# Queue orders in a two-layer RWKV-7 and gated-MLP trunk: w_o splits, LoRA weights, block weights

## The chip, the cores and the metric

The kernel runs on one core of a Trainium2 chip. The metric is the device time of one execution, in microseconds (us). A core has five engines with a queue each, worked off in order: PE (TensorE: matmuls and transposes), DVE (VectorE), ACT (ScalarE), POOL (GpSimd) and SP (SyncE, which here issues nearly all DMAs). Engines wait for one another by semaphores only, so an instruction that waits holds up everything behind it in its own queue.

## The reference

Input x is (1, 512, 1024) in float32. Two layers, each a token mixer and a dense feed-forward part, each with an RMS norm in front and another behind it:

```python
for i in range(DEPTH):                       # 2
    h = _rmsnorm(x, norm_gains[i, 0])
    h = rwkv_time_mix(h) if i == 0 else sgu_mixer(h)
    x = x + _rmsnorm(h, norm_gains[i, 1])
    h = _rmsnorm(x, norm_gains[i, 2])
    h = (silu(h @ w_gate) * (h @ w_up)) @ w_down      # 1024 -> 2816 -> 1024
    x = x + _rmsnorm(h, norm_gains[i, 3])
```

The first mixer is an RWKV-7 time mixing: the norm's output and its shift by one token are mixed and projected to r, k and v; two small LoRA products (w1, a1) give decay and a; then for each of 16 heads a state is carried over 512 tokens, `S = S diag(w) + (S a) b^T + v k^T`, `y = S r`, a group norm, a bonus, a gate, and the output projection `(y * g) @ w_o`. The second mixer is a gated MLP over blocks of 128 positions.

## The kernel before, in words

**Precision.** Matmuls that must be exact to float32 are made as three fp32r products: a weight is loaded raw, ScalarE casts it to a high part, VectorE subtracts that for the low part (`split`, L177 to L180; `weight`, L182 to L200, does load and split). So each weight tile costs a DMA on SP, a cast `whi` on ACT (L179), a subtraction `wlo` on DVE (L180), and PE's `mm3` (L204) follows. `weight` loads into `wraw`, two buffers; a load waits until the buffer's last tile has been split.

**Order.** Python traces the program; then a scheduler, which runs a simulated timeline, fixes the order of every engine's instructions. An instruction that is ready early in the simulation may be issued ahead of others that were traced before it. Two calls bind this order without adding a wait: `tc.issue_after(ins)` queues what a block traces on the engine of `ins` behind `ins`; `tc.keep_in_program_order(ins)` queues `ins` behind the one instruction traced just before it on its engine.

**The time mixing.** `rwkv` (from L528) first normalizes the four row tiles (L588 to L602: square sums on ACT, a reciprocal root in single-element steps on DVE, L256 to L258, scaling, PE transposes, gains), then scales the LoRA weights w1 by the mixing vectors: `w1m[0]` by 1 - mix on DVE and `w1m[1]` by mix on POOL (L645). The 16 LoRA matmuls (L649; the trace shows 32) take `w1m[0]` first. Then the 16 heads are worked in four groups of four, by a plan written out by hand:

```python
PLAN = "P0 E0 P1 E1 P2 E2 P3 E3 X0 F0 B0 F1 V0 V1 V2 V3 B1 S0 F2 S1 F3 N0 B2 N1 B3 S2 N2 S3 N3".split()
```

P projects k and r, E makes the decays, V projects v, F and B build the chunk matrices (`back`, B, inverts triangular blocks: a loop of 15 pairs of small DVE steps on `Dm`, then two 32x32 block transposes `Dn` and `Dt` (L911, L912), transposes of MV on PE copied to `MVt` by ACT (L922), and PE steps Qp, Np, Tp, Q2p, T2p, mp and gh with copies between them), S is the scan over eight chunks (PE `us`, L1005, then a copy `su` on DVE and ACT, then the next `us`), N the group norm, bonus and gate. `B3` is called "inverse 3" here, S3 "scan 3". The output of the groups goes through DRAM (`od`) to the output projection.

**The output projection.** `out_proj` (L273) has two column halves and four weight units a half (`unit`, L289), a unit being 2 k tiles x 4 token tiles x 3 products = 24 matmuls. In this call (`spare=e2`, L1151) half 0 takes `whi` and `wlo` from two buffers, half 1 from a pool of its own. The weights w_o don't depend on anything, so the scheduler places their loads, casts and subtractions where its timeline has room. Two units are cast and subtracted before 260 us, three between 336 and 362 us, the rest from 438 us on.

**The feed-forward part.** `ffn` first works two column groups plainly (`plain`, 8 weights through `wraw`), then the other nine in blocks by Strassen's scheme: seven products a group (p1 to p7) from four weight quarters a11, a12, a21, a22. `quad` (L362) loads a quarter of gate and of up by two DMAs of 256 KB into one tile `wq`, whose buffers rotate over three tags (`wraw`, `f0`, `gain`), two each, that other parts use as well. The order of these loads on SP is the scheduler's: in the first layer four quarters are issued ahead of the plain groups' last weights, the first of them at 417.64 us, within scan 3, and later on a quarter whose buffer is free goes ahead of one traced earlier that still waits for its buffer.

Of the kernel before, what the change touches and what calls it, by code (L numbers as in the profile page):

```python
# [11 lines left out]
ALU = mybir.AluOpType  # L12

P = 128
T = 512
D = 1024
KT = D // P
# [113 lines left out]
class Trunk:  # L131
# [138 lines left out]
    def prenorm(self, col):  # L270
        return Norm(self, col)

    def out_proj(self, acts, wrows, nk, row, xts, store=None, tail=3, norm=None, spare=None, mid=None):  # L273


        nc = self.nc
        v = nc.vector
        gain = self.bcast_row(row)
        nu = nk // 2
        cols = [slice(0, 512), slice(512, 1024)]  # L280
        late = (1, 1) if spare else (0, tail)
        accs, f0, part = [None, None], [], []

        def mms(half, k, tt, w):
            tok = slice(tt * P, (tt + 1) * P)
            hi, lo = acts(k)
            self.mm3(accs[half][tt], (hi[:, tok], lo[:, tok]), w, k == 0, k == nk - 1)

        def unit(half, u):  # L289
            own = spare if half and u < nu - late[1] else None  # L290
            hi, lo = self.weight(wrows(u)[:, :, cols[half]], spare=own)
            return [(2 * u + j, (hi[:, j, :], lo[:, j, :])) for j in range(2)]

        def first(half):
            accs[half] = self.accs(half)
            for u in range(nu - late[half]):
                for k, w in unit(half, u):
                    for tt in range(TT):
                        mms(half, k, tt, w)

        def post0(tt, junk):
            acc = accs[0][tt]
            s = self.sumsq(acc, junk)
            if tt % 2 == 0:
                f0.append(self.f0p.tile([P, 2, 512], F32, name="f0", tag="f0", bufs=2))
            v.tensor_tensor(f0[-1][:, tt % 2, :], acc, gain[:, cols[0]], op=ALU.mult)
            part.append(self.part(s, 1.0 / D, RMS_EPS))
            if tt == (0 if spare else TT - 1):
                nc.scalar.activation(junk[:, 0:1], part[tt][0], AF.Sqrt)

        def post1(tt, hn):
            acc, lo, hi = accs[1][tt], hn[:, 0:512], hn[:, 512:1024]
            s = self.sumsq(acc, lo)
            v.tensor_tensor(hi, acc, gain[:, cols[1]], op=ALU.mult)
            y = self.rsqrt1(s, part[tt], 1.0 / D)
            for f, c in ((f0[tt // 2][:, tt % 2, :], cols[0]), (hi, cols[1])):
                v.scalar_tensor_tensor(xts[tt][:, c], f, y[:, 0:1], xts[tt][:, c], op0=ALU.mult, op1=ALU.add)
                if store is not None and tt == TT - 1:
                    nc.sync.dma_start(out=store[tt * P:(tt + 1) * P, c], in_=xts[tt][:, c])
            if store is not None and tt < TT - 1:  # L320
                nc.sync.dma_start(out=store[tt * P:(tt + 1) * P, :], in_=xts[tt])

        hn_tile = lambda: self.sm.tile([P, D], F32, name="hn", tag="hn", bufs=2)
        first(0)
        if not spare:
            for tt in range(TT):
                post0(tt, hn_tile()[:, 0:512])
        if mid:
            mid()
        first(1)  # L330
        ends = [[kw for u in range(nu - late[half], nu) for kw in unit(half, u)] for half in range(2)]
        for tt in range(TT):
            for half in range(2):
                for k, w in ends[half]:
                    mms(half, k, tt, w)
            if norm and tt >= LAG:
                norm.step(tt - LAG, xts[tt - LAG])
            hn = hn_tile()
            if spare:
                post0(tt, hn[:, 512:1024])  # L340
            post1(tt, hn)
        if norm:
            for tt in range(TT - LAG, TT):
                norm.step(tt, xts[tt])
            norm.finish()
# [5 lines left out]
    def ffn(self, li, xts, norm, store=None, nxt=None, early=()):  # L351
        nc = self.nc
        early = list(early)
        v, a = nc.vector, nc.scalar
# [4 lines left out]
        acts, pairs, loads, seeded = [], {}, [0], []  # L359
        g, u = slice(0, 256), slice(256, 512)  # L360

        def quad(n, j, f):  # L362
            pool, tag = ((self.wp, "wraw"), (self.f0p, "f0"), (self.gp, "gain"))[loads[0] % 3]
            loads[0] += 1
            t = pool.tile([P, 2, 4, P], F32, name="wq", tag=tag, bufs=2)
            for m, w in enumerate(wgu):
                nc.sync.dma_start(out=t[:, m], in_=w[:, 4 * j:4 * j + 4, (2 * n + f) * P:(2 * n + f + 1) * P])
            return t

        def product(ps, name, src, start=False):  # L370
# [15 lines left out]
        def p1(n):  # L386
            o = pairs[n] = dict(act=self.slot([P, 2, T], F32, "act"))
            acts.append(o["act"])
            o["a11"] = quad(n, 0, 0)
            o["R"] = self.bank("R", "R")  # L390
            product(o["R"], 1, o["a11"], True)
            if len(seeded) < 2:
                q = self.bank("Q", "Q")
                seeded.append(q)
                bh = b[1][0]
                nc.tensor.matmul(q, bh[:, 0, 0:P], bh[:, 0:2].rearrange("p k t -> p (k t)"), start=True, stop=True)
            o["Q"] = seeded[(n - PLAIN) % 2]
            a.copy(o["Q"], o["R"])
# [9 lines left out]
        def p2(n):  # L408
            o = pairs[n]
            o["a12"] = quad(n, 1, 0)  # L410
            product(o["R"], 2, o["a12"])
            gate(o["act"][:, 0, g], o["R"])
# [113 lines left out]
    def rwkv(self, x0):  # L526
        nc, i, tc = self.nc, self.i, self.tc
        v, a, g = nc.vector, nc.scalar, nc.gpsimd  # L528
        mm = nc.tensor.matmul
        with ExitStack() as ctx:  # L530
# [17 lines left out]
            def s4(name, shape, dt=F32):  # L548
                return self.slot(shape, dt, name)
# [4 lines left out]
            def gslot(name, shape):  # L554
                return self.gp.tile(shape, F32, name=name, tag="gain", bufs=2)
# [25 lines left out]
            w1 = s4("w1", [P, KT, 2, 64])  # L581
# [32 lines left out]
            omix = rp.tile([P, 48], F32, name="omix")  # L614
# [25 lines left out]


            w1m = [s4("w1m", [P, KT, 2, 64]) for _ in range(2)]
            for t, m, w in ((w1m[0], omix, v), (w1m[1], self.vec["mix"], g)):
                mv = m[:, 3 * KT:5 * KT].rearrange("p (j k) -> p k j", j=2).unsqueeze(3)
                w.tensor_tensor(t, w1, mv.broadcast_to([P, KT, 2, 64]), op=ALU.mult)  # L645
            acc = self.bank("pt", "lora")
            for j, src in enumerate((hk, hs)):
                for kt in range(KT):
# [98 lines left out]
            full = lambda t: t.rearrange("p b r -> p (b r)")[:, 0:1024].rearrange("p (t s) -> p t s", s=32)  # L747
# [135 lines left out]
            def back(b, o):  # L883

                MV, BX, LA, Dm = (o[n] for n in ("MV", "BX", "LA", "Dm"))
# [16 lines left out]
                for j in range(15):  # L902
                    n = 15 - j
# [5 lines left out]
                Dt = rp.tile([P, 16, 2, 32], F32, name="Dt", tag="hid", bufs=1)  # L909
                Dn = self.sm.tile([P, 16, 2, 32], F32, name="hn", tag="hn", bufs=2)  # L910
                v.transpose(Dn.rearrange("p u x s -> p s (u x)"), full(Dm).rearrange("p t s -> p s t"))  # L911
                v.transpose(Dt.rearrange("p u x t -> p t (u x)"), full(Dm))  # L912
                MVt = {}
                for hh in range(2):
                    mt = gslot("MVt", [P, 2, 4, P])
                    for q in q2:
                        pt = self.bank("pl", "mvt")
                        for cc in range(4):
                            nc.tensor.transpose(pt[:, cc * P:(cc + 1) * P], MV[hh, q][:, cc, 0].rearrange("p h t -> p (h t)"),
                                                self.ident)  # L920
                        MVt[hh, q] = mt[:, q]
                        a.copy(mt[:, q].rearrange("p c f -> p (c f)"), pt)  # L922

                quarters = [(64 * hd + 32 * x, hd, x) for hd in q2 for x in q2]
                Qp = self.bank("pt", "Qp")
# [40 lines left out]
                for hh, q in units:  # L966
                    mp, mt, mv, bx = self.bank("mp" if b else "pt", "mp"), MVt[hh, q], MV[hh, q], BX[hh, q]
# [137 lines left out]
            xr, kr, ops, Y = None, {}, {}, {}  # L1105
            for n in PLAN:
                f, b = n[0], int(n[1])
# [38 lines left out]
            xts = [self.xp.tile([P, D], F32, name="x", tag="x", bufs=TT) for _ in range(TT)]  # L1146
            for t in range(TT):
                nc.sync.dma_start(out=xts[t], in_=i["x"][0, t * P:(t + 1) * P, :])
            wo = i["rwkv_w_o"][0].rearrange("(u j p) n -> u p j n", p=P, j=2)
            norm = self.prenorm("g02")  # L1150
            self.out_proj(acts, lambda u: wo[u], KT, i["norm_gains"][0, 1], xts, norm=norm, spare=e2)  # L1151
            return xts, norm


# [134 lines left out]
```

## Time and profile before

| what | before |
|---|---|
| median of 3 runs | 1358.06 us (1356.09 to 1360.63) |
| the profiled execution, its own time | 1356.2 us |
| its span, first to last instruction | 1354.5 us |
| mean granted TensorE clock | 0.979 |
| matmuls | 9812 |
| DMA | 140.10 MB, 103 GB/s on the mean |

How to read a profile: times are microseconds from the start of the span. A row of the chain of waits has a start, a duration and what lay on the chain. A row of a timeline has a start, a duration, engine, line, operation, output <- inputs, shapes and count, and in brackets how long its engine sat idle before it and what ended that. A row of a group has count, busy time, mean ns of one, and idle time before. A row of a table by stretches has the stretch, its length, then busy time and instructions of PE, PEld (weight loads), DVE, ACT and POOL, the granted clock as a share of full speed, the share of the DMA engines and their GB/s. SPq is SP's queue of DMA issues.

### The profile page before, as it was taken

How to read it: one execution, taken by the hardware profiler on the slowest of the kernel's cores; microseconds unless marked ns; L12 is line 12 of the kernel's file. 1: busy time of each engine (PE TensorE's matmuls, PEld its weight loads, DVE VectorE, ACT ScalarE, POOL GpSimd, SP SyncE). 2: the span in 40 equal slices, each digit the busy share in tenths (PEclk: the TensorE clock that was granted, in tenths of full speed). 3: DMA queues.
4: the chain of work that ended last, by engine and by line, in shares of the span. 5: the costliest groups of instructions: out<-in, count | busy, mean ns of one | idle time of the engine just before them, and what ended most of it. 6: DMA issues, size and time to landing. Idle time of an engine off the chain costs nothing.

```text
span 1354.5 us, 24545 instructions
## 1 busy us (share of the span) xinstructions
PE 1285.7 (95%) x9812; PEld 1116.5 (82%) x9812; DVE 897.0 (66%) x1519; ACT 694.1 (51%) x1240; POOL 179.1 (13%) x307
## 2 busy tenths in 40 slices
PE   5989999989799889999999999999989999999997
PEld 3657789887677688999998887878888999998886
DVE  7865676477847489878785225575679777785223
ACT  7975785576433375455464223643454454464221
POOL 1000175566100033000000002020002000000000
PEclk9989999999799989999999999999989999999999
DMA  5136596322214232433323332243520433323321
GB/s 158 39 85 158 135 212 176 110 74 64 85 46 136 86 102 78 125 112 107 98 78 121 93 110 80 94 148 99 157 78 16 125 109 95 109 63 124 94 93 62
DMA packets 217266, 140.10 MB, mean 103 GB/s; under 512 B 67856, under 2 KB 193344, under 8 KB 217152
## 3 DMA queue, kind: packets, MB, share of 16 engines
q1 hardware_dynamic: 215856, 133.81, 34.2%
q0 software_dynamic: 1296, 4.72, 1.0%
q8 instruction: 77, 1.26, 0.4%
q14 instruction: 37, 0.30, 0.1%
HBM read 124.35 MB, written 14.16 MB: 102 GB/s over the span
## 4 chain that ended last, share of the span: by engine, by line
PE 78%; DVE 9%; ACT 5%; DMA 4%; issue 2%; SPq 1%; POOL 0%; DVEq 0%; ACTq 0%
PE acc L204 26%; PE Q L204 10%; PE Z L204 7%; PE proj L204 6%; PE R L204 6%; PE gu L204 4%; PE u L204 3%; PE v L204 3%; PE gh L976 2%; DMA wq<-in_ffn_w_up_dram 2%; PE lm L861 2%; DVE wlo L180 2%; PE lora L649 1%; PE mp L969 1%; DVE wsum L383 1%
## 5 line engine op out<-in xcount | busy, mean ns | idle before, releaser
L180 DVE TENSOR_TENSOR wlo<-wraw,whi 128x1024 fp32r<-128x1024 f32 x109 | 133.7, 1227 | 195.4 <-ACT whi L179 191.5
L179 ACT CAST whi<-wraw 128x1024 fp32r<-128x1024 f32 x109 | 114.3, 1048 | 227.6 <-PE acc L204 142.0
L204 PE MATMUL acc<-whi,actw 128*128 128x512 f32 x704 | 220.8, 394 | 0.0
L204 PE MATMUL Q<-bc,whi 128*128 128x256 f32 x864 | 156.8, 282 | 1.7 <-ACT hn L427 1.7
L204 PEld LDWEIGHTS acc<-whi,actw 128*128 128x128 f32 x704 | 132.3, 188 | 30.6
L204 PE MATMUL acc<-wlo,actw 128*128 128x512 f32 x352 | 138.6, 394 | 0.0
L204 PEld LDWEIGHTS Q<-bc,whi 128*128 128x128 f32 x864 | 133.4, 190 | 2.5 <-ACT hn L427 2.3
L204 PE MATMUL Q<-bc,wlo 128*128 128x256 f32 x432 | 121.7, 282 | 1.1 <-DVE wlo L180 1.1
L179 ACT CAST whi<-wsum 128x1024 fp32r<-128x1024 f32 x72 | 75.2, 1051 | 84.5 <-PE Q L204 30.1
L204 PE MATMUL Z<-bc,whi 128*128 128x256 f32 x576 | 105.8, 282 | 0.7 <-ACT whi L179 0.7
L204 PE MATMUL R<-bc,whi 128*128 128x256 f32 x576 | 105.0, 281 | 0.0
L180 DVE TENSOR_TENSOR wlo<-wsum,whi 128x1024 fp32r<-128x1024 f32 x72 | 86.9, 1221 | 19.1 <-ACT whi L179 18.6
L204 PE MATMUL gu<-hT,whi 128*128 128x256 f32 (+1 forms) x384 | 92.6, 335 | 2.4 <-DVE hT L62 1.4
L204 PE MATMUL proj<-xsp,whi 128*128 128x512 f32 x256 | 85.6, 413 | 5.5 <-ACT xsp L179 3.1
L204 PEld LDWEIGHTS Z<-bc,whi 128*128 128x128 f32 x576 | 88.9, 189 | 1.1 <-ACT whi L179 0.9
L204 PEld LDWEIGHTS R<-bc,whi 128*128 128x128 f32 x576 | 88.9, 188 | 0.2
L180 DVE TENSOR_TENSOR wlo<-wq,whi 128x1024 fp32r<-128x1024 f32 x54 | 69.2, 1282 | 28.1 <-ACT whi L179 28.0
L179 ACT CAST whi<-wq 128x1024 fp32r<-128x1024 f32 x54 | 56.7, 1050 | 59.6 <-PE R L204 17.6
L204 PEld LDWEIGHTS Q<-bc,wlo 128*128 128x128 f32 x432 | 81.9, 190 | 1.5 <-DVE wlo L180 1.5
L204 PE MATMUL R<-bc,wlo 128*128 128x256 f32 x288 | 80.9, 281 | 0.0
L204 PE MATMUL Z<-bc,wlo 128*128 128x256 f32 x288 | 80.7, 281 | 0.1
L204 PEld LDWEIGHTS acc<-wlo,actw 128*128 128x128 f32 x352 | 66.1, 188 | 15.3
(346 smaller groups left out, 2858.7 us busy)
## 6 DMA issues: line engine op xcount, KB each, us to landing
wraw<-in_ffn_w_down_dram SPq DMA_DIRECT2D x44, 512.0 KB
wq<-in_ffn_w_gate_dram SPq DMA_DIRECT2D x72, 256.0 KB
wq<-in_ffn_w_up_dram SPq DMA_DIRECT2D x72, 256.0 KB
wraw<-in_rwkv_w_rkv_dram SPq DMA_DIRECT2D x24, 512.0 KB
wraw<-in_sgu_w_in_dram SPq DMA_DIRECT2D x16, 512.0 KB
x<-in_x_dram SPq DMA_DIRECT2D x8, 512.0 KB
ST<-sb SPq DMA_DIRECT2D x8, 512.0 KB
MV<-sa SPq DMA_DIRECT2D x32, 128.0 KB
```

The lines of the kernel that those rows point to most:

```text
L179: self.nc.scalar.copy(hi, src)
L180: self.nc.vector.tensor_tensor(lo, src, hi.bitcast(F32), op=ALU.subtract)
L204: self.nc.tensor.matmul(out, l, r, start=start, stop=stop, skip_group_check=resumed)
L383: v.tensor_tensor(s, x, y, op=ALU.add)
L649: mm(acc, w1m[j][:, kt].rearrange("p j n -> p (j n)"), src(kt), start=j == 0 and kt == 0, stop=j == 1 and kt == KT - 1)
L861: mm(lm[:, cc * P:(cc + 1) * P], st[:, cc].rearrange("p n t -> p (n t)"), mv[:, cc, :, hd, :], start=True, stop=True)
L969: mm(mp[:, cc * P:(cc + 1) * P], bdT[:, q * NC + 4 * hh + cc].rearrange("p h t -> p (h t)"), mt[:, cc, :], start=True, stop=True)
L976: mm(gh[:, cc * P:(cc + 1) * P], mt[rows, cc, :], bx[rows, 0:2, cc, :], start=True, stop=True)
```

## The change

Three orders are bound; no work is added or taken away but for one multiplication that changes its engine.

```diff
-    def out_proj(self, acts, wrows, nk, row, xts, store=None, tail=3, norm=None, spare=None, mid=None):
+    def out_proj(self, acts, wrows, nk, row, xts, store=None, tail=3, norm=None, spare=None, mid=None, after=()):
...
         def unit(half, u):
             own = spare if half and u < nu - late[1] else None
-            hi, lo = self.weight(wrows(u)[:, :, cols[half]], spare=own)
+            with ExitStack() as order:
+                for ins in after:
+                    order.enter_context(self.tc.issue_after(ins.ins))
+                hi, lo = self.weight(wrows(u)[:, :, cols[half]], spare=own)
...
             for m, w in enumerate(wgu):
-                nc.sync.dma_start(out=t[:, m], in_=w[:, 4 * j:4 * j + 4, (2 * n + f) * P:(2 * n + f + 1) * P])
+                load = nc.sync.dma_start(out=t[:, m], in_=w[:, 4 * j:4 * j + 4, (2 * n + f) * P:(2 * n + f + 1) * P])
+                self.tc.keep_in_program_order(load)
...
-            for t, m, w in ((w1m[0], omix, v), (w1m[1], self.vec["mix"], g)):
+            for t, m in ((w1m[0], omix), (w1m[1], self.vec["mix"])):
                 mv = m[:, 3 * KT:5 * KT].rearrange("p (j k) -> p k j", j=2).unsqueeze(3)
-                w.tensor_tensor(t, w1, mv.broadcast_to([P, KT, 2, 64]), op=ALU.mult)
+                tc.keep_in_program_order(v.tensor_tensor(t, w1, mv.broadcast_to([P, KT, 2, 64]), op=ALU.mult))
...
-                v.transpose(Dt.rearrange("p u x t -> p t (u x)"), full(Dm))
+                o["turned"] = v.transpose(Dt.rearrange("p u x t -> p t (u x)"), full(Dm))
...
-                        a.copy(mt[:, q].rearrange("p c f -> p (c f)"), pt)
+                        o["copied"] = a.copy(mt[:, q].rearrange("p c f -> p (c f)"), pt)
...
-            self.out_proj(acts, lambda u: wo[u], KT, i["norm_gains"][0, 1], xts, norm=norm, spare=e2)
+            self.out_proj(acts, lambda u: wo[u], KT, i["norm_gains"][0, 1], xts, norm=norm, spare=e2, after=(ops[3]["turned"], ops[3]["copied"]))
```

`after` names two instructions of `back(3)`: the Dt transpose on DVE and the last of the four MVt copies on ACT. So in the time mixing's output projection all casts on ACT are queued behind that copy and all subtractions on DVE behind that transpose; the DMAs on SP are on neither engine and stay free. The other output projections get no `after`. Both w1m multiplications run on DVE, the first behind the instruction traced before it on DVE (`omix`, L615), the second behind the first. Each of the 144 wq loads of the two feed-forward parts is queued on SP behind the DMA traced just before it.

## The prediction

> **What bounds the kernel now.** I read the page first, then the stretches cut by stage, then the chain of waits and the engines' timelines at the three places that the change touches.
>
> ```profile
> span 1354.5 us, 24545 instructions
> PE 1285.7 (95%) x9812; PEld 1116.5 (82%) x9812; DVE 897.0 (66%) x1519; ACT 694.1 (51%) x1240; POOL 179.1 (13%) x307
> PE 78%; DVE 9%; ACT 5%; DMA 4%; issue 2%; SPq 1%; POOL 0%; DVEq 0%; ACTq 0%
> ```
>
> PE is busy for 95% of the span and carries 78% of the chain. So a change of queue orders can only win back stretches where PE has no work or runs at a lower clock: 1354.5 - 1285.7 = 68.8 us in all, plus what the clock costs.
>
> ```profile
> core 0: us, PE busy (x) PEld busy (x) DVE busy (x) ACT busy (x) POOL busy (x), PEclk, DMA share, GB/s
> 22.00:62.00 40.00, 40.00 (x131) 23.60 (x132) 35.03 (x51) 34.48 (x58) 0.00 (x0) 1.00 0.13 38
> 336.00:366.00 30.00, 21.54 (x386) 17.40 (x380) 27.23 (x61) 14.43 (x25) 6.13 (x12) 0.77 0.33 101
> 366.00:382.00 16.00, 15.15 (x123) 12.72 (x127) 9.18 (x24) 5.01 (x11) 0.00 (x0) 0.79 0.13 42
> 382.00:412.00 30.00, 27.79 (x673) 24.45 (x662) 13.50 (x31) 12.15 (x32) 1.15 (x3) 1.00 0.17 50
> 412.00:445.00 33.00, 29.40 (x204) 22.13 (x204) 24.67 (x72) 12.98 (x28) 0.00 (x0) 1.00 0.51 160
> 500.00:550.00 50.00, 50.00 (x324) 45.06 (x322) 46.09 (x49) 26.36 (x31) 14.64 (x4) 1.00 0.22 65
> 550.00:590.00 40.00, 38.09 (x314) 37.21 (x314) 29.62 (x30) 16.95 (x23) 0.00 (x0) 1.00 0.50 143
> 590.00:712.00 122.00, 122.00 (x1029) 121.81 (x1028) 96.39 (x103) 64.55 (x88) 1.14 (x2) 1.00 0.33 96
> 1050.00:1080.00 30.00, 28.21 (x234) 27.63 (x233) 23.40 (x24) 14.23 (x20) 0.00 (x0) 1.00 0.49 138
> 348.00:360.00 12.00, 9.36 (x94) 7.70 (x92) 10.57 (x38) 4.73 (x7) 0.00 (x0) 0.50 0.13 44
> ```
>
> The stretch to look at is 336 to 366 us (group norm 1, the middle of inverse 2, all of inverse 3's VectorE loop). PE works 21.54 of 30 us, and from 348 to 360 at half clock, while VectorE is busy 27.23 of 30: here VectorE is the bound. The blocks' steady part (590 to 712) has PE busy throughout, so there is nothing to win in it. At the two block starts PE lacks 1.91 us (550 to 590) and 1.79 us (1050 to 1080).
>
> **Part 1, the output projection's splits.** All eight ScalarE casts (whi) go behind inverse 3's last MVt copy, all eight VectorE subtractions (wlo) behind its Dt transpose. The loads on SP are not bound by this. The chain of waits in the VectorE-bound stretch:
>
> ```profile
> 339.61 1.11 DVE wlo L180
> 340.74 3.73 DMA wraw<-in_rwkv_w_o_dram
> 344.49 1.05 ACT whi L179
> 345.57 1.23 DVE wlo L180
> 346.82 3.65 DMA wraw<-in_rwkv_w_o_dram
> 353.42 1.87 PE T2p L960 x64
> ```
>
> The chain goes through w_o for 1.11 + 3.73 + 1.05 + 1.23 + 3.65 = 10.77 us, but VectorE had other work during most of it, and that is what is late next. The groups of the stretch (VectorE) and its waits, then the two instructions that the splits are queued behind:
>
> ```profile
> L180 DVE TENSOR_TENSOR wlo<-wraw,whi 128x1024 fp32r<-128x1024 f32 x3 | 3.6, 1207 | 0.2 <-ACT whi L179 0.2
> ACT whi L179 <- DMA wraw<-in_rwkv_w_o_dram: 1.6, 2, 1.1
> 364.27 1.89 DVE L912 STREAM_TRANSPOSE Dt<-Dm 128x1024 f32<-128x1024 f32 x1
> 381.10 1.07 ACT L922 COPY MVt<-mvt 128x512 f32<-128x512 f32 x2
> ```
>
> Three subtractions leave: 3 x 1.207 = 3.6 us, and 0.2 us of waiting for a cast. What is left for VectorE is 27.23 - 3.6 = 23.6 us; with the 2.77 us in which it idled unchanged, the stretch is 3.6 us shorter, without any idle it would be 6.4 us shorter, and if the stretch were bound by PE's chain alone it would gain nothing. I take -4.0: near the first, since ScalarE's two waits for DMA (1.6 us) go too and let inverse 2's bdT copies and T2p (353.42) come earlier. The clock I leave as it is: PE still has holes there.
>
> Two earlier casts leave as well. One stands on the chain, ahead of the copies that POOL's masks wait for:
>
> ```profile
> 252.38 0.94 ACT whi L179
> ```
>
> Between 0 and -0.94; I take the middle, -0.5.
>
> What comes back: five casts and subtractions (two from before 260 us, three from 336 to 362) now stand between 375 and 440 us, in inverse 3's second half and scans 2 and 3. A subtraction there is 1.2 us by the row above, a cast 1.05. VectorE has room (13.50 of 30 and 24.67 of 33 busy), but both queues are in order: behind a cast that waits for its load stand the scan's su copies, and the scan's next matmul waits for those. Bounds: 0, and 5 x 1.2 + 5 x 1.05 + 1.6 of DMA waits = 12.9 if every one stood on the path. PE is without work in 2.21 + 3.60 of these 63 us, 9%, and 9% of 12.9 is 1.2; I take +1.5. PE's filler there is the output projection itself:
>
> ```profile
> 383.35 3.88 PE acc L204 x16
> 393.26 2.05 PE acc L204 x8
> ```
>
> Only one unit's 24 matmuls (3.88 + 2.05 = 5.93 us) run before 412, so two units split right behind the copies are early enough; the price if they aren't is a rival below. Sum of part 1: -4.0 - 0.5 + 1.5 = -3.0.
>
> **Part 2, the LoRA weights.** VectorE and POOL at the start:
>
> ```profile
> 13.19 0.18 DVE L615 TENSOR_SCALAR omix<-vecT 128x48 f32<-128x48 f32 x1
> 14.01 1.23 DVE L645 TENSOR_TENSOR w1m<-w,omix 128x1024 f32<-128x1024 f32 x1 [0.46 <-DMA w<-in_rwkv_a_dram]
> 15.15 1.89 DVE L257 SCALAR_TENSOR_TENSOR rt<-rr,rm 128x1 f32<-128x1 f32 x1
> 14.06 2.97 POOL L645 TENSOR_TENSOR w1m<-w,vecT 128x1024 f32<-128x1024 f32 x1 [10.43 <-DMA w<-in_rwkv_a_dram]
> 21.90 15.89 PE lora L649 x32
> ```
>
> rt is an operation on one element a partition, and it lasts 1.89 us, to the moment when POOL's 2.97 us multiply ends (14.06 + 2.97 = 17.03). It lies on the last row tile's norm, so on the way to the first LoRA matmul at 21.90. Without POOL some 1.8 us go. VectorE gets 1.23 us more. The pin binds the first multiply only behind omix, which it reads anyway and which already ran at 13.19, so nothing says that the norm's last steps come first. If both multiplies run in front of rt the gain is 1.8 - 1.2 = 0.6 us; if the second runs under the LoRA matmuls (its product is wanted at the 17th of 32) it is 1.8. Worst, the loss is 1.2, if rt was late for another reason. I take -1.2. It is kept, since PE has no gap from 22 to 62 us (40.00 of 40).
>
> **Part 3, block weights in order.** Every wq load is queued on SP behind the load traced before it. Today four of them are issued ahead of the plain groups' weights. The first, with what waits beside it, and the places where VectorE waits for a block load now:
>
> ```profile
> 417.64 0.37 SPq L367 DMA_DIRECT2D wq<-in_ffn_w_gate_dram  x1
> 422.50 1.29 DVE L1052 TENSOR_TENSOR hn<-hn,bn 128x512 f32<-128x512 f32 x2 [3.12 <-DMA hn<-Vd]
> 516.68 0.37 SPq L367 DMA_DIRECT2D wq<-in_ffn_w_gate_dram  x1
> 548.77 0.37 SPq L367 DMA_DIRECT2D wq<-in_ffn_w_gate_dram  x1
> 534.79 2.35 DVE L383 TENSOR_TENSOR wsum<-wq 128x1024 f32<-128x1024 f32 x2
> 550.28 4.69 DMA wq<-in_ffn_w_up_dram
> 555.10 1.23 DVE L383 TENSOR_TENSOR wsum<-wq 128x1024 f32<-128x1024 f32 x1 [1.85 <-DMA wq<-in_ffn_w_up_dram]
> 1053.86 1.22 DVE L383 TENSOR_TENSOR wsum<-wq 128x1024 f32<-128x1024 f32 x1 [2.44 <-DMA wq<-in_ffn_w_up_dram]
> ```
>
> At 417.64 the load leaves scan 3, where 512 KB less is in flight beside V and the scan's su loads. hn was issued ahead of it, so at most a part of the 3.12 us belongs to it: 0 to -3.1, I take -0.3. The first six tiles then leave SP together from 516.68 on. Two tiles take from 548.77 to 550.28 + 4.69 = 554.97 to land, 3.1 us each; the sixth would be there 6 x 3.1 = 18.6 us later, at 535.3, and its first use, the second of two sums, starts 1.2 us after 534.79. PE has no gap from 500 to 550 (50.00 of 50), which hides it; with that cover gone it would cost one tile, 3.1 us. A new order has one more price: n=3's a21 waits for a slot that n=2's a11 gives back late, and a22, whose slot is free earlier and which is issued ahead today, stands behind it. Each block start can so lose 3.1 us, or win back what it loses now (1.91 and 1.79 us) if the VectorE waits shown (1.85 and 2.44) go. I take 0 for both. SP's other loads pass: nothing of scan 3 is traced behind a wq load, and those who waited behind one only gain.
>
> **Sum.** -3.0 - 1.2 - 0.3 = -4.5 us against the profiled execution's 1356.2: 1351.7. The median of the runs before is 1358.06, 1.9 above that execution, so the forecast for a median is 1353.5. A measurement of this kernel tells about 0.3% (4.1 us) from no change.
>
> **The rivals.** *The clock stays up.* PE ran 9.36 us of work at 0.50 from 348 to 360; at full clock it takes half, and 4.7 us go. For it: the slow stretch follows the two waits for w_o on the chain (340.74 and 346.82). Against it: inverse 2's copies still make PE wait there, and from 366 to 382, with PE busy 15.15 of 16 us, the clock is low as well (0.79). Result -4.5 - 4.7 = -9.2: 1349. The Trainium skill (TensorE: Matmul & The Clock Gate, What's actually happening) says that the clock is halved after an idle window of about 3.4 us and comes back after a busy one as long. By that rule the hole need only shrink below the window, and the time is this rival's; the trace agrees in that the clock is halved where PE lacks work, and shows nothing on where the threshold lies.
>
> *The stalls move.* The casts wait for their loads in scans 2 and 3 as they do now in inverse 3, and part 1's 4.0 us come back there: -0.5, 1357.6. For it: the loads aren't bound, two wraw buffers serve eight units, and a load takes 3.7 us. Against it: PE is 92% busy there with other work.
>
> *The splits come too late (slower).* If the first unit isn't ready when PE reaches it at 383, the 5.93 us of filler run later in one piece and inverse 3's matmuls run bare, and each of the next two units waits for a load (3.73) and a cast (1.05): 5.93 + 2 x 4.78 = 15.5, less the 1.5 that I have counted, so -4.5 + 14.0 = +9.5: 1367.6. It decides from 8.6 us on: so much more than counted must PE wait for w_o between 382 and 445 for the change to end 4.1 us slower. Against it: the copies that the casts wait for (381.10) come earlier by part 1's own gain.
>
> *It does little.* The scheduler may place the instructions about as before at the start and in the blocks; that leaves part 1, -3.0, inside the forecast's own range.
>
> **How the numbers follow.** Forecast 0.46 (its own range, -8 to -1: 1350 to 1357), clock 0.18, stalls move 0.22, splits late 0.14. Faster by over 0.3% means under 1354.0: the clock case and some two thirds of the forecast (0.31), 0.49. Slower means over 1362.1: the late splits and a little of the in-order loads (two tiles of 3.1 us on top of moved stalls), 0.16. The rest, 0.35, is the same. The range leaves out the far halves of the clock case and of the late splits: 1345 to 1363.
>
> **What would show it.** Right: no wlo or whi of w_o between 230 and 370 us; the stretch from inverse 2's Tp to inverse 3's Dt about 4 us shorter; rt at 0.2 us and the LoRA matmuls starting near 20.7; wq loads only behind the plain groups' weights, PE still without a gap behind them. Wrong: PE waiting for whi or wlo of w_o in scans 2 and 3, ScalarE casts there behind DMA waits of several us, a LoRA start that hasn't moved, or PE gaps over 2 us at either block start behind the second wsum.

## The result and the profile after

| what | before | after |
|---|---|---|
| median | 1358.06 us (1355.38 to 1360.63, 5 runs) | 1347.22 us (1345.89 to 1350.03, 5 runs) |
| ratio after / before | | 0.9926, 95% interval 0.9904 to 0.9948 |
| profiled execution, its span | 1354.5 us | 1344.2 us |

The change is 10.8 us faster by the medians, 10.3 us by the two spans. The top of the page of after:

```profile
span 1344.2 us, 24525 instructions
PE 1279.7 (95%) x9812; PEld 1115.3 (83%) x9812; DVE 898.5 (67%) x1520; ACT 694.9 (52%) x1240; POOL 166.3 (12%) x306
```

PE does the same 9812 matmuls. It is without work for 1344.2 - 1279.7 = 64.5 us in place of 68.8, and busy 6.0 us less (a busy PE is not PE at its peak). To see where, I follow landmarks through both traces (start times in us; a stretch runs from one start to the next; "Tp of inv. 2" is its first Tp; inverse 3's `Dt` begins its second half, the last `Yp` ends the scans; the first and the last `yb` open the two feed-forward parts):

| | first Qp | Tp of inv. 2 to Dt of inv. 3 | Dt of inv. 3 to last Yp | last Yp | first yb | last yb |
|---|---|---|---|---|---|---|
| before | 230.8 | 26.5 | 68.2 | 432.5 | 501.5 | 1012.4 |
| after | 218.9 | 20.2 | 77.6 | 425.4 | 491.0 | 1002.5 |

11.9 us are won before the first Qp, ahead of everything that part 1 touches. Part 1's stretch is 6.3 us shorter, but the stretch behind it 9.4 us longer. Five of the prediction's stretches, in after:

```profile
core 0: us, PE busy (x) PEld busy (x) DVE busy (x) ACT busy (x) POOL busy (x), PEclk, DMA share, GB/s
22.00:62.00 40.00, 38.75 (x130) 23.59 (x130) 35.55 (x56) 35.28 (x58) 0.00 (x0) 0.96 0.16 46
336.00:366.00 30.00, 27.48 (x401) 23.75 (x395) 23.80 (x62) 11.77 (x23) 0.00 (x0) 0.79 0.08 27
366.00:382.00 16.00, 11.61 (x314) 9.20 (x314) 8.84 (x13) 9.84 (x20) 0.41 (x2) 0.80 0.51 155
500.00:550.00 50.00, 46.33 (x291) 41.92 (x291) 45.71 (x45) 22.04 (x28) 6.58 (x4) 0.97 0.43 119
1050.00:1080.00 30.00, 30.00 (x254) 30.00 (x254) 23.93 (x25) 14.23 (x19) 0.00 (x0) 1.00 0.50 137
```

PE has 5.94 us more work in the VectorE-bound stretch, 3.54 less right behind it, a gap at the first feed-forward block and none at the second. (The work reaches these stretches some 10 us earlier than before, so only stretches moved along with it compare exactly; that is done below.) VectorE's timeline at the LoRA weights (a line of "..." marks rows left out):

```profile
13.85 1.23 DVE L649 TENSOR_TENSOR w1m<-w,omix 128x1024 f32<-128x1024 f32 x1 [0.21 <-DMA w<-in_rwkv_a_dram]
14.99 1.22 DVE L649 TENSOR_TENSOR w1m<-w,vecT 128x1024 f32<-128x1024 f32 x1
16.13 0.21 DVE L257 SCALAR_TENSOR_TENSOR rt<-rr,rm 128x1 f32<-128x1 f32 x1
...
16.87 1.22 DVE L180 TENSOR_TENSOR wlo<-wraw,whi 128x1024 fp32r<-128x1024 f32 x1 [0.46 <-ACT whi L179]
...
18.35 0.15 DVE L258 SCALAR_TENSOR_TENSOR ry<-rt,rr 128x1 f32<-128x1 f32 x1
```

Both multiplies stand ahead of rt, which takes 0.21 us as foretold. But the norm's last ry now stands behind a weight split, and the LoRA matmuls start at 23.25 us, 1.35 us *later* than before. So the 11.9 us can't have come by the way that the prediction gave.

### The profile page after: what moved, and what is told of

Same layout as the page of the kernel before. It is cut to its first block, busy times and chain, and to the rows that moved or that the text cites. A ratio compares the mean times of both kernels' runs of the same rounds, so it can differ in the third digit from the quotient of the medians.

```text
span 1344.2 us, 24525 instructions
## 1 busy us (share of the span) xinstructions
PE 1279.7 (95%) x9812; PEld 1115.3 (83%) x9812; DVE 898.5 (67%) x1520; ACT 694.9 (52%) x1240; POOL 166.3 (12%) x306
## 4 chain that ended last, share of the span: by engine, by line
PE 58%; DVE 5%; ACT 1%; issue 1%; DMA 0%; SPq 0%; DVEq 0%; ACTq 0%
PE acc L204 24%; PE Q L204 11%; PE Z L204 7%; PE R L204 7%; PE gu L204 5%; PE u L204 3%; DVE wlo L180 1%; DVE wsum L387 1%; PE s L1227 1%; PE ptr L267 0%; ACT whi L179 0%; DVE braw L106 0%; DVE hT L62 0%; DVE bc L180 0%; DVE x L320 0%
## 5 line engine op out<-in xcount | busy, mean ns | idle before, releaser
L204 PEld LDWEIGHTS acc<-whi,actw 128*128 128x128 f32 x704 | 132.3, 188 | 30.7
L180 DVE TENSOR_TENSOR wlo<-wsum,whi 128x1024 fp32r<-128x1024 f32 x72 | 87.0, 1220 | 20.3 <-ACT whi L179 19.1
L204 PE MATMUL proj<-xsp,whi 128*128 128x512 f32 x256 | 82.4, 401 | 1.3 <-ACT r L674 1.3
```

The source lines that it names most:

```text
L180: self.nc.vector.tensor_tensor(lo, src, hi.bitcast(F32), op=ALU.subtract)
L204: self.nc.tensor.matmul(out, l, r, start=start, stop=stop, skip_group_check=resumed)
```

## The experiments

All totals are ratios to before with 95% intervals; "us" behind them is the ratio times 1358. A profile is one execution: before itself ran between 1350.7 and 1367.5 us in the 77 runs beside the experiments. How far one order can vary is seen in the third experiment: its queues have the order of before up to its first block load at about 417 us, and still its last T2p starts at 405.4 us, before's at 397.1. Much of this difference is the granted clock: the stretch from 367 to 386 us, all of it under before's order, ran at half clock in e3 with PE busy throughout (the row below), where before has a mean of 0.82.

```profile
core 0: us, PE busy (x) PEld busy (x) DVE busy (x) ACT busy (x) POOL busy (x), PEclk, DMA share, GB/s
367.00:386.00 19.00, 19.00 (x92) 15.79 (x92) 8.07 (x20) 4.38 (x11) 0.00 (x0) 0.50 0.17 54
```

So totals are judged by the ratios, and stages by differences that several kernels repeat.

| | ratio | us | first Qp | Tp to Dt | Dt to Yp |
|---|---|---|---|---|---|
| e1 splits | 1.0051 (1.0025 to 1.0078) | +6.9 | 230.3 | 20.0 | 91.4 |
| e2 LoRA | 0.9925 (0.9904 to 0.9947) | -10.2 | 221.2 | 34.3 | 65.5 |
| e3 block loads | 1.0027 (1.0006 to 1.0048) | +3.7 | 230.0 | 26.3 | 75.9 |
| e4 splits, LoRA | 0.9945 (0.9924 to 0.9965) | -7.5 | 220.0 | 20.3 | 78.5 |
| e5 r splits first | 0.9986 (0.9959 to 1.0012) | -1.9 | 227.3 | 25.6 | 70.0 |
| e6 second half's splits | 0.9970 (0.9941 to 0.9998) | -4.1 | 229.7 | 20.3 | 79.5 |
| e7 as e6, with LoRA | 0.9910 (0.9878 to 0.9943) | -12.2 | 220.4 | 27.3 | 66.3 |
| e8 LoRA, block loads | 0.9944 (0.9915 to 0.9972) | -7.6 | 221.2 | 30.2 | 65.7 |
| e9 LoRA's order, POOL | 0.9937 (0.9914 to 0.9959) | -8.6 | 220.4 | 34.2 | 65.6 |
| e10 before's order, VectorE | 1.0012 (0.9992 to 1.0033) | +1.6 | 229.8 | 25.8 | 65.7 |
| e11 LoRA's order to 95 us | 0.9958 (0.9937 to 0.9980) | -5.7 | 222.9 | 26.7 | 69.6 |
| e12 as e7, second block's loads | 0.9909 (0.9888 to 0.9930) | -12.4 | 221.3 | 26.7 | 66.6 |

**Each part alone, and the first two (e1 to e4).** e1 has only the hunks of `out_proj`, `turned` and `copied`; e3 only those of `quad`; e4 is the full change without `quad`'s. e2 is this alone:

```diff
-            for t, m, w in ((w1m[0], omix, v), (w1m[1], self.vec["mix"], g)):
+            for t, m in ((w1m[0], omix), (w1m[1], self.vec["mix"])):
...
-                w.tensor_tensor(t, w1, mv.broadcast_to([P, KT, 2, 64]), op=ALU.mult)
+                tc.keep_in_program_order(v.tensor_tensor(t, w1, mv.broadcast_to([P, KT, 2, 64]), op=ALU.mult))
```

> Only the first part: the output projection's weight splits behind inverse 3's Dt transpose and last MVt copy; the LoRA weights and the block loads as before. The prediction's theory (the splits leave a stretch bound by VectorE): -3.0 us, so about 1355; no gain ahead of 219 us, since nothing of this part touches it; Tp of inverse 2 to Dt of inverse 3 about 4 us shorter. The rival (the whole gain comes from the LoRA multiply, whose move lets the projections run in another order): between -1 and +2 us, 1357 to 1360, with first Qp still near 230.8 us. A third theory (any added order shuffles the queues and the gain is chance) would allow -10.

> Only the second part: both LoRA weight multiplies on VectorE. The prediction's theory (rt no longer waits for POOL): -1.2 us, 1356.9, with first Qp near 229.6 us. The rival (the projections run in another order): first Qp near 219 us, 12 us earlier than before, and a total of -9 to -13 us, 1345 to 1349; the VectorE-bound stretch from 336 us stays as long as it was. If the splits were needed for the gain: within 2 us of before.

> Only the third part: the block loads in order. The prediction: -0.3 us, 1357.8, each block start within -1.9 to +3.1 us. From the trace of the full change the rival says: the first block's start (500 to 550 us) loses about 4 us, since PE then waits for weights there, and the second's (1050 to 1080) wins about 2, in all +2 us, 1360. Up to 400 us the landmarks stand where they stood before.

> The first two parts, the block loads as before. The prediction's theory: -4.2 us, 1353.9. The rival (the LoRA multiply's order carries the gain, the loads in order lose 4 us at the first block and win 2 at the second): about 2 us better than the full change, -13 us, 1345. If the splits take back what the LoRA part won in the inverses: no better than the LoRA part alone.

The LoRA part alone gives what the full change gives. The splits alone are slower, and so are the loads in order. The singles add up to +6.9 - 10.2 + 3.7 = +0.4 us, the full change gave -10.0 by its ratio: the parts don't add.

e1 shows how the splits lose. ScalarE's waits for w_o's loads from 366 to 400 us, and the chain of waits there:

```profile
ACT whi L179 <- DMA wraw<-in_rwkv_w_o_dram: 8.0, 3, 3.4
```

```profile
373.73 5.87 DMA wraw<-in_rwkv_w_o_dram
379.62 1.05 ACT whi L179
380.70 1.24 DVE wlo L180
381.95 3.83 DMA wraw<-in_rwkv_w_o_dram
385.80 1.06 ACT whi L179
386.88 1.24 DVE wlo L180
388.14 3.83 DMA wraw<-in_rwkv_w_o_dram
391.98 1.04 ACT whi L179
393.05 0.52 ACT su L1013 x2
393.62 0.45 PE us L1008 x8
```

This is the prediction's slower rival, step by step. A raw buffer comes free only when the subtraction before it is done, so each next load starts late; the cast waits for it, and the scan's su stands behind the cast on ScalarE. In this execution (1368.5 us, one of e1's longer ones) the clock was low behind that, too. The stretch in e1, then in before:

```profile
core 0: us, PE busy (x) PEld busy (x) DVE busy (x) ACT busy (x) POOL busy (x), PEclk, DMA share, GB/s
395.00:425.00 30.00, 29.95 (x155) 26.20 (x156) 14.79 (x39) 6.72 (x16) 0.74 (x1) 0.50 0.33 104
```

```profile
395.00:425.00 30.00, 29.45 (x339) 24.67 (x338) 16.57 (x46) 10.09 (x26) 1.15 (x3) 1.00 0.41 125
```

PE is busy nearly throughout in both, at half clock in e1. The group of gh matmuls from 396 to 420 us has a mean of 438 ns in e1; in before, from 400 to 412 us, it has 286:

```profile
L979 PE MATMUL gh<-BX,MVt 64*128 64x128 f32 x48 | 10.3, 438 | 0.1
```

```profile
L976 PE MATMUL gh<-BX,MVt 64*128 64x128 f32 x50 | 5.6, 286 | 0.0
```

That the held splits caused this is not shown: e3 has such a stretch without them. Over all 11 executions of e1 that its ratio rests on, the granted clock is 0.9756 on the mean, beside 0.9773 of before's 23: as an estimate 0.0017 x 1360 = 2.3 of the 6.9 us, if PE had work throughout.

**One edge in the E stage (e5).** Before's ScalarE casts the last r features behind the E stage's logarithm, a table load and several activations, and PE waits for them. e5 binds only that; `held[0]` is the cast of the last r split:

```diff
-                a.activation(flat(ri), flat(ri), AF.Ln, bias=tiny[:, 1:2])
+                with ExitStack() as order:
+                    if b == 0:
+                        order.enter_context(tc.issue_after(held[0].ins))
+                    a.activation(flat(ri), flat(ri), AF.Ln, bias=tiny[:, 1:2])
```

> Before, with one order added and nothing else: in the E stage of pair 0 the logarithm on ScalarE (and with it its table load and the inverse root behind it) goes behind ScalarE's cast of the last split of the r features. Theory of the feature splits (what the LoRA part won is that ScalarE's and VectorE's splits of the r features no longer stand behind the E stage's activations, so that PE doesn't wait 3.08 and 1.77 us for them near 80 us and keeps its clock from 80 to 90 us): between 77 and 90 us PE's gaps shrink to under 2 us and the clock goes from 0.66 to 0.9 or more; first Qp 5 to 8 us earlier than 230.8; total -5 to -8, 1349 to 1353. Rival (the LoRA part won by its other changes of order or by POOL's being free): the same gap appears elsewhere before 220 us, and the total is within 2 us of before, 1355 to 1360.

The wait did not go, it moved. PE's longest wait from 20 to 222 us in e5 and, for the same place, two in before:

```profile
PE proj L204 <- ACT r L670: 4.0, 1, 4.0
```

```profile
PE proj L204 <- ACT xsp L179: 3.1, 1, 3.1
PE proj L204 <- DVE xsp L180: 1.8, 1, 1.8
```

The copy of the r projection now stands behind the logarithm. From 77 to 90 us PE is still without work for 4.42 us (under 2 was expected), at a clock of 0.75. First Qp came 3.5 us earlier, the total -1.9 with an interval that holds 0: the expected 5 to 8 us are missed. One edge isn't the cause; the next two pairs ask whether the whole order is.

**Order against engine (e9, e10).** The order of every queue is written out in the kernel (`ORDER`: for PE, DVE, ACT, POOL and SP the names of another kernel's queue, in order), e9 with the order of e2, e10 with that of before:

```diff
+def in_written_order(tc):
+    traced = {i.name: i for i in tc.nc.cur_bb.bb.instructions}
+    for queue in ORDER.values():
+        queue = [f"I-{n}" for n in queue if f"I-{n}" in traced]
+        for a, b in zip(queue, queue[1:]):
+            tc.add_manual_dep(traced[b], a, mybir.DependencyInfo(mybir.DependencyClass.NoSync, mybir.DependencyReason.DATA),
+                              reason="written order")
```

> The code of before, the second LoRA multiply on POOL as before, but every queue (PE, VectorE, ScalarE, POOL, SP) pinned to the order that the kernel with the LoRA part alone has. Theory of the order (the LoRA part's gain is the new order of the queues, not POOL's multiply): first Qp near 221 us in place of 230.8, total -8 to -11, 1347 to 1350, ratio to before about 0.993. Theory of the engine (POOL's 2.97 us multiply slows VectorE, or comes late): rt lasts 1.9 us again, total within 2 us of before, 1356 to 1360.

> The other way round: both LoRA multiplies on VectorE, one behind the other, and every queue pinned to the order of before. Theory of the order: rt 0.2 us, but first Qp at 229 to 231 us and the total within 2 us of before, 1356 to 1360. Theory of the engine: first Qp near 221 us and -8 to -11, 1347 to 1350. The prediction's own term, in its place: -1.2, with the LoRA matmuls starting up to 1.2 us earlier than 21.9.

In the traces, the rows of ScalarE and SyncE stand in e9 in the order of e2 and in e10 in that of before, all of them; on VectorE and POOL the one multiply is the only difference. With POOL's multiply in place and only the order exchanged, 8.6 us are won (e9). With both multiplies on VectorE and before's order, nothing is (e10: +1.6, the interval holds 0). The Qp rows of before, e9 and e10:

```profile
L928 PE MATMUL Qp<-hn,LA x512: 184/191/212, 230.8 to 382.9; 32*32 32x32 f32 x171
```

```profile
L931 PE MATMUL Qp<-hn,LA x512: 184/191/212, 220.4 to 370.4; 32*32 32x32 f32 x171
```

```profile
L931 PE MATMUL Qp<-hn,LA x512: 184/191/212, 229.8 to 379.5; 32*32 32x32 f32 x171
```

And the LoRA weights of e9 (VectorE and POOL), then of e10:

```profile
15.19 1.89 DVE L260 SCALAR_TENSOR_TENSOR rt<-rr,rm 128x1 f32<-128x1 f32 x1
```

```profile
14.09 2.97 POOL L648 TENSOR_TENSOR w1m<-w,vecT 128x1024 f32<-128x1024 f32 x1 [10.46 <-DMA w<-in_rwkv_a_dram]
```

```profile
16.16 0.21 DVE L260 SCALAR_TENSOR_TENSOR rt<-rr,rm 128x1 f32<-128x1 f32 x1
```

The faster e9 still has rt at 1.89 us, the slower e10 has it at 0.21. So the stall that the prediction priced is real, and taking it away gains nothing that shows in the total (at most 1.1 us by the interval). In ScalarE's timelines one sees what the order does. First e10 (before's order), then e9 (the LoRA kernel's):

```profile
70.87 1.28 ACT L801 ACT_TABLE_LOAD   x1
...
73.94 1.28 ACT L771 ACT_TABLE_LOAD   x1
...
77.95 0.61 ACT L182 CAST xsp<-xs 128x512 fp32r<-128x512 f32 x1
...
79.18 0.61 ACT L182 CAST xsp<-xs 128x512 fp32r<-128x512 f32 x1
```

```profile
71.27 0.62 ACT L182 CAST xsp<-xs 128x512 fp32r<-128x512 f32 x1
...
72.36 0.62 ACT L182 CAST xsp<-xs 128x512 fp32r<-128x512 f32 x1
...
75.38 1.28 ACT L801 ACT_TABLE_LOAD   x1
...
77.73 1.03 ACT L182 CAST whi<-wraw 128x1024 fp32r<-128x1024 f32 x1
78.67 0.58 ACT L673 COPY r<-proj 128x512 f32<-128x512 f32 x1
79.26 1.28 ACT L783 ACT_TABLE_LOAD   x1
```

The last feature splits, which PE needs next, stand behind two table loads and the E stage's activations in the one, ahead of both in the other; and a weight cast and the r copy (77.73 and 78.67) now stand between the two loads, too.

**How much of it is the first stretch (e11).** The edit is the function above, with the LoRA kernel's order for the first 338 matmuls, 158 instructions of ScalarE and of VectorE each and 56 of SyncE, and before's from there.

> The code of before, the second LoRA multiply on POOL; the queues in the order of the LoRA kernel up to about 95 us alone (338 matmuls on PE, 158 instructions on ScalarE and on VectorE, 56 on SP), and in the order of before from there on. If the gain comes from the first features and PE's gap between 77 and 90 us: gap under 3 us, clock 0.85 or more there, first Qp at 225 us or earlier, total -4 to -8, 1350 to 1354. If it comes from the order behind 95 us: first Qp at 229 or later, total within 2 us of before.

The stretch from 77 to 90 us in before, e9 and e11:

```profile
77.00:90.00 13.00, 7.55 (x20) 4.80 (x20) 9.69 (x13) 9.20 (x14) 0.00 (x0) 0.74 0.00 1
```

```profile
77.00:90.00 13.00, 10.66 (x39) 8.33 (x40) 8.60 (x10) 12.01 (x15) 0.00 (x0) 0.87 0.36 105
```

```profile
77.00:90.00 13.00, 10.27 (x37) 8.01 (x38) 8.21 (x10) 12.38 (x16) 0.00 (x0) 0.87 0.34 99
```

PE's time without work falls from 5.45 to 2.34 us in e9 and 2.73 in e11, and the clock rises from 0.74 to 0.87. First Qp is at 222.9 in e11, the total -5.7: by the ratios the order up to 95 us gives two thirds of e9's 8.6 us. The intervals of e9 and e11 overlap, so what the order behind 95 us adds is not measured. Gap and clock of this stretch make up 3.1 + 0.13 x 13 = 4.8 of the 10.4 us by which e9's first Qp comes earlier (an estimate from the rows); the rest is not traced to a place.

**The second half's splits alone (e6, e7).** To part e1's late loads from its other prices, only the units of the second column half are held; the first half's two early units are split before 260 us as before:

```diff
-                for ins in after:
+                for ins in after if half else ():
```

> Before, with the first part for the second half's three units alone: the first half's two early units are split where they were (before 260 us), so that PE has 48 matmuls of filler ready at inverse 3, and both raw buffers are loaded long before the held casts. Theory of the late loads (the splits alone lost since two units were cast late, their raw buffers came free late, and ScalarE then waited 8.0 us for the next units' loads with the scan's copies queued behind): ScalarE's waits for w_o between 366 and 400 us fall from 8.0 to under 4 us; the gain up to Dt of inverse 3 is kept at least in half (-5 or more); last Yp at or before 432; total -3 to -7, 1351 to 1355. Rival (any w_o cast behind inverse 3 holds up scans 2 and 3, or PE's low clock there has another cause): last Yp at 440 or later, total +3 to +8, 1361 to 1366.

> The second part (LoRA multiplies on VectorE) with the first part for the second half's units alone, block loads as before. If the LoRA part's gain lies before 220 us and the held second half wins in the inverses, the two add up: -13 to -16, 1342 to 1345, better than the full change. If the held second half wins nothing, it is the LoRA part's own time, 1348; if it loses as the whole first part did, 1352 to 1355.

e6 is 11 us better than e1 (-4.1 against +6.9, the intervals lie apart), with ScalarE's waits for w_o halved, 4.0 us in place of 8.0 (under 4 was expected). That speaks for the late loads. But one expectation failed: the last Yp is at 437.7, not by 432, so holding them still lengthens that stretch (79.5 us from Dt to Yp; the kernels with no held split have 65.5 to 75.9). With the LoRA part (e7) the total is -12.2; the stretch to Dt is shorter than in e2 (27.3 against 34.3) and the one behind it isn't longer (66.3). The intervals of e7 and e2 overlap, so a gain over the LoRA part alone is not shown.

**The block loads with the LoRA part, and in the second block alone (e8, e12).** e8 has the LoRA hunk and `quad`'s. e12 is e7 with

```diff
+                if li:
+                    self.tc.keep_in_program_order(load)
```

> The second and third part, the output projection's splits as before. Alone the third part cost 3.7 us by its ratio; between the first two parts and the full change it won about 2.6. If its price doesn't depend on the rest: -10.2 + 3.7 = -6.5, 1351.5. If it depends on which loads stand in its way and wins behind the LoRA part as in the full change: -12 to -13, 1345.

> The LoRA part, the splits of the second half's units alone behind inverse 3, and block loads in order in the second feed-forward block alone, where PE's gaps fell from 1.8 to 0 us with the third part by itself (the first block keeps the order of before, where the full change left PE 3.7 us without work from 500 to 550 us). If the three add up: -12.2 - 2 = -14, 1344, with PE busy throughout from 1040 to 1090 us. If the loads' order wins nothing here: as without it, -12, 1346.5. If they cost as they did alone: -9, 1349.

e8 lies between its two expectations (-7.6 against -6.5 and -12), nearer to a price that doesn't depend on the rest. In stretches moved along with yb (90 us from 1.5 us ahead of the first yb, 80 us from 2.4 us ahead of the last), PE's busy time is 88.09 and 78.21 us in before, 85.83 and 80.00 in e3, 86.98 and 76.92 in e4, 84.43 and 80.00 in after: in these two pairs the order costs 2.3 to 2.6 us at the first block and wins 1.8 to 3.1 at the second. Beside e2 (86.70 and 77.32), e8 (85.46 and 77.10) loses 1.2 at the first and wins nothing at the second, and that stays open. The first block's gap has other causes as well: e7, whose loads have no bound order, has 85.25 there. e12 has the second block's gain (80.00 in place of e7's 78.43):

```profile
1050.00:1080.00 30.00, 30.00 (x255) 30.00 (x254) 23.97 (x25) 14.56 (x20) 0.00 (x0) 1.00 0.51 140
```

With 0.9909 it is the fastest of all, 1345.37 us as a median, but its interval overlaps those of e7, e2 and the full change: the version points the right way and isn't shown to be better.

## Why the prediction was right and wrong

The forecast (1353.5) said faster, and the measured 1347.22 lies in the range of 1345 to 1363, but below the forecast's own range of 1350 to 1357. The reason it gave is not what happened: as far as its argument goes, that the change came out faster was luck.

**Part 2 is where it failed.** The step was "Without POOL some 1.8 us go", for -1.2, taken as the edit's only effect. e10 measures that step with both multiplies in front of rt: rt is 0.21 us, and the LoRA matmuls start at 21.23 in place of 21.90, near the 0.6 us that the prediction gave for this case (e1, e3, e5 and e6, with POOL's multiply, start at 21.5 to 21.7, so part of it is spread). The total doesn't gain (+1.6, -1.1 to +4.5). Its reason for being kept, "PE has no gap from 22 to 62 us", fell too: in e10 PE has 39.00 of 40 busy there. What the sum lacked was any price for re-sorting. The scheduler lays the queues out along a simulated timeline, so one multiply on another engine gave every queue another order; that order alone is -8.6 (e9). The prediction mentioned the scheduler only as a way for the change to do less. The rows to look at were in the trace of before: the two waits of PE near 80 us and the clock of 0.74, outside of the parts that I costed. The pin was no part of it: the instruction lists with and without `keep_in_program_order` on the multiplies are the same.

**Part 1: the first half was right and larger, the second was mis-sized.** No whi or wlo of w_o is left between 230 us and Dt in after, and Tp to Dt is 6.3 us shorter where 4.0 was taken; e1, e4 and e6 agree (20.0 to 20.3 against 26.5). That is close to the prediction's bound of 6.4, "without any idle": in this stretch VectorE's work falls from 24.2 to 19.5 us, and its idle time from 2.3 to 0.7. The term that failed is "I take +1.5" for what comes back, with "two units split right behind the copies are early enough" behind it. The first two are early enough, at 370 to 373 us in e1; the next three wait for their loads. From Dt to the last Yp e1 gives back 23.2 us, e6 11.3, after and e4 9.4 and 10.3. Part of this is the clock, which is 0.95 in this stretch in before, 0.79 in e1, 0.91 in e6, 0.95 in after and 0.93 in e4. Length times clock (an estimate, as if PE had work throughout) is 64.8 us in before, 62.2 in e3 and 63.5 in e2, which hold no split, 63.0 in e7, and 72 to 74 in e1, e4, e6 and after. So by this estimate the term is some 7 to 9 us, and what e1 has beyond that is its clock. The slower rival named this mechanism with 14.0 us and 8.6 us as the point from which it decides; e1 alone came out on its side (+6.9, where part 1 would have cost -3.0 + 14.0 = +11.0 in it). The two low rows that I trusted, VectorE's 13.50 of 30 and PE's 9% idle, say how full the engines are, not what stands behind a wait. Behind the LoRA part the same hunk costs about 2.7 us by the ratios (e4 against e2; their intervals overlap). The sign that the prediction named as wrong, ScalarE casts behind waits for loads, stands in after as well, from 366 to 400 us:

```profile
ACT whi L179 <- DMA wraw<-in_rwkv_w_o_dram: 5.8, 3, 3.4
```

The -0.5 for the cast at 252 us was not measured by itself.

**Part 3** was taken at 0 for the block starts. Measured in PE's busy time it is -1.6 to -3.1 at the second in three of four pairs and nothing in the fourth (the bound given was 1.79), and +1.2 to +2.6 at the first in three, inside the 3.1. The first has the sign named as wrong, a gap over 2 us behind the second wsum, which waits for a load. VectorE's and PE's timelines of after:

```profile
538.06 2.36 DVE L387 TENSOR_TENSOR wsum<-wq 128x1024 f32<-128x1024 f32 x2 [2.09 <-DMA wq<-in_ffn_w_up_dram]
```

```profile
541.61 0.38 PE L204 MATMUL Z<-bc,wlo 128*128 128x256 f32 x1 [2.35 <-DVE wlo L180]
```

The cover of "PE has no gap from 500 to 550" was a property of the old order, and went with it. The wait for hn, of which -0.3 was expected, is 2.11 us in e3 in place of 3.12. e3's +3.7 as a whole is more than these two; the rest isn't traced to a place.

**The rivals.** In the stretch that the rival of the clock named, it did not stay up: 0.79 from 336 to 366 us in after, 0.77 before. Both profiled executions have a mean of 0.979, but they are one execution each. Over all executions it is 0.9804 in after's five and 0.9766 in before's 77; 0.9822 in e2 beside 0.9773, 0.9791 in e9 beside 0.9768. The difference times the 1350 us, an estimate, is some 5 us for after, 7 for e2 and 3 for e9. So a good part of the gain is clock, but won elsewhere; the one place shown is 77 to 90 us (0.74 to 0.87). "It does little" had the right premise turned round: the scheduler did move instructions, and that was the gain.

## What to carry to other kernels

Where a scheduler lays out the queues, an edit's first effect may be the new layout: compare the order of all queues before costing the edit, and to test a reason, exchange order and edit separately, as e9 and e10 do. Work that is moved behind an event must have its load already landed, for a cast that waits on an in-order queue holds up whatever that queue owes to the critical loop. Holding back only the part that PE needs last did better than holding back all (e6 against e1).

## What the runs showed of the hardware

The half clock does not end when the profile shows PE busy: in e1 PE worked 29.95 of 30 us from 395 to 425 us at 0.50, in e3 19.00 of 19 us from 367 to 386, and in before the same gh matmuls as in e1 ran at 1.00 from 400 us on. In the clock records of all the traces here, every stretch at half clock that ends within the program lasts 3.4 us or a multiple of it (6.8 from 80 us in before, 20.5 from 366 in e3, 30.7 from 394 in e1). The Trainium skill (TensorE: Matmul & The Clock Gate, What's actually happening) has the full clock come back after a sustained busy window of about 3.4 us; these two stretches do not agree with it. What the chip counts as busy there, none of these runs shows.
